# Fifty input projections as twenty-five seven-product units, and a bitwise search for the top 256 on ScalarE

## The chip, the core and the metric

One NeuronCore of a Trainium2 chip runs one program. TensorE (PE) multiplies, with its weight loads (PEld) shown apart; VectorE (DVE), ScalarE (ACT) and GpSimd (POOL) do the rest; SyncE (SP) issues nearly all DMAs. The program holds one list of instructions for each engine; an instruction may name counters of other engines, or of its own, that have to be reached before it starts. The metric is device time in microseconds for one execution, lower is better, taken as the median of several runs.

## The reference, cut to what matters

```python
D_MODEL, SEQ, DEC_BATCH, TOP_K_MAX, Q_BLOCK = 1024, 1024, 8, 256, 128    # T = 8 + 1024 token columns in the kernel
def trunk_layer(x, conv_prev, attend, mem_k, mem_v, lw):
    h = rms_norm(x, g_mix)
    z = jnp.einsum('btd,de->bte', h, w_in)
    (c_in, c_b, c_c, q, k, v, iq, ik, iw, gate_a, gate_b) = jnp.split(z, splits, axis=-1)
    conv_out, conv_state = short_conv(c_c * c_in, conv_prev, conv_w)          # 3 taps
    out_a = jnp.einsum('btc,cd->btd', c_b * conv_out, w_conv_out)
    attn = attend(q, k, v, iq, ik, iw)
    out_b = jnp.einsum('bte,ed->btd', attn, w_attn_out)
    x = x + jnp.einsum('btd,de->bte', sigmoid(gate_a) * out_a + sigmoid(gate_b) * out_b, w_o)
    x = x + memory_attend(rms_norm(x, g_mem), mem_k, mem_v, w_mq, w_mo)
    h = rms_norm(x, g_ffn)
    f = jax.nn.silu(h @ w_gate) * (h @ w_up)
    return x + f @ w_down
def indexer_topk(iq, iw, ik, q_pos, top_k):
    score = einsum('bths,bth->bts', relu(einsum('bthd,bsd->bths', iq, ik)), iw) * IDX_SCALE
    _, idx = lax.top_k(where(causal, score, NEG_INF), top_k)   # attention then sees these 256 keys alone
```

Widths of z in columns: c_in, c_b, c_c, q, gate_a and gate_b 1024 each, k and v 256 each, iq 256, ik 64, iw 4. Everything is float32 to the outside.

## The kernel before

Every float32 operand is held as a high and a low part ("split": ACT copies the high part, POOL or DVE subtracts it to get the low part), and a product is three matmuls: high by high, high by low, low by high. Activations stand transposed, 128 features on the partitions by T = 1032 tokens. SBUF is 48 slots of 1040 floats (`Slots`), handed out in the order in which they came free.

The stages run one after the other on PE: memory keys and values; the index keys and queries ik and iq; nine tiles of v; the index scores of the query blocks 7 to 2 against up to 1024 keys; the input projections; attention; the output and memory-attention products; the feed-forward.

`dense(8, h)` makes one 128-row output of a projection: 8 blocks by 3 products by 3 chunks of 344 columns, 72 matmuls. The input projections are 50 such calls (c_in, c_c and c_b 8 times each, then gate_a, gate_b, k, q), with w_conv_out between them as 32 calls of `dense(2)` that add into eight accumulators (L791). PSUM banks 0 to 5 serve two calls in turn. The results leave PSUM on ACT or DVE after each call; k and q are split and stay in SBUF. After each call `bg.pump(budget)` writes a piece of a background generator into the queues, so many microseconds' worth by costs noted in the generator.

The background work here is `topk()` (L747): for two query blocks at a time 32 rounds of MAX8 (L752) and MATCH_REPLACE8 (L755) on DVE, then a mask. After it comes `sample_index()`, small work for the eight decode tokens. Four index-score pieces of attention (`pre_score`) are hooked into the last q calls.

The feed-forward already uses another form. `unit()` (L1622) makes two 128-row outputs for all 1032 tokens with seven quarter-size products instead of eight (Strassen's scheme in Winograd's form): each product is 4 blocks by 3 matmul kinds by 2 chunks of 258 columns, so a unit is 168 matmuls of 258 columns. It needs sums of quarters of the weights (`UnitWeights.sums`, L226 to L229 on DVE), their splits (`high` L236 on ACT, `low` L244 on DVE) and sums of the activations, made once by `x_sums` and `x_last` (L1586 to L1620). After each of its products 1 to 7 something is taken out of PSUM or prepared for the next unit:

```python
if j == 0:   ACT.copy(c2(half(p1, 0)), psum(0))                 # and split W, Y; load the next unit
elif j == 2: V.tensor_tensor(c2(half(ca, 1)), psum(1), ...)     # bank pair is written again by product 5 (j = 4)
elif j == 3: ACT.copy(...) or V.tensor_tensor(...)              # then UW.sums(u + 1)
elif j == 4: two V.tensor_tensor                                # then UW.high(u + 1, "U")
```

Of the kernel before, what the change touches and what calls it, by code (L numbers as in the profile page):

```python
# [8 lines left out]
F32 = mybir.dt.float32  # L9
# [14 lines left out]
NSLOT = 48  # L24
# [22 lines left out]
def weight_plan():  # L47
# [149 lines left out]
class UnitWeights:  # L197


    def __init__(self, nc, slots, ws):  # L200
        self.nc, self.slots, self.ws = nc, slots, ws
        self.n = ws.shape[0]
# [36 lines left out]
    def low(self, u, x):  # L239
        if u >= self.n:  # L240
            return
        w = 512 if x == "Y" else 1024
        raw, (h,), l = self.raw[u].pop(x), self.hl[u, x], self.slots.get(F32R)
        self.nc.vector.tensor_tensor(l[0][:, :w], raw[0][:, :w], h[0].bitcast(F32)[:, :w], op=ALU.subtract)  # L244
        self.slots.put(raw)
        self.hl[u, x] = h, l

    def operand(self, u, x, q):
        k, i = W_SIDE[x]
        c = 512 * i + 128 * q  # L250
        return [t[0][:, c:c + 128] for t in self.hl[u, k]]
# [64 lines left out]
def build(tc, A):  # L316
# [17 lines left out]
    W = Weights(nc, S, A["ws"])  # L334
    bg = Background()
# [83 lines left out]
    m8 = const.tile([128, 2, 8], F32, name="m8")  # L419
# [77 lines left out]
    def split_ps(ps, between=None):  # L497
# [5 lines left out]
        return h, l  # L503

# [88 lines left out]
    for half in range(2):  # L593
        for kp in range(4):
# [3 lines left out]
            for p in range(3):  # L598
                for kk in range(2):
# [1419 lines left out]
```

## Time and profile before

| | us |
|---|---|
| median of 3 runs (2142.87 to 2146.04) | 2145.67 |
| the profiled execution's own time | 2149.56 |
| its span, first to last instruction | 2147.8 |
| PE busy in the span | 2099.0 |
| DVE, ACT, POOL busy | 1281.1, 621.8, 605.5 |

A dense call is 72 matmuls of 344 columns, a unit 168 of 258 columns. Each view lists instructions under the line of kernel.py that made them; helper lines (L470 for `dense`, L1643 for `unit`) stand for many stages, so stages are told apart by time: v tiles 108 to 134 us, scores 134 to 159, input projections 159 to 790, feed-forward units 1470 to 1881.

### The profile page before, as it was taken

The page shows a single profiled execution, that of the slowest core. Times are in us where ns is not written, and L with a number is a line of the kernel's source. Part 1 is how long each engine was busy: PE and PEld are TensorE (multiplying, and loading weights), DVE is VectorE, ACT ScalarE, POOL GpSimd, SP SyncE. Part 2 cuts the span into 40 slices and gives each one's busy share as a digit, 9 for nine tenths or more (in the row PEclk, how much of TensorE's full clock was granted, in tenths as well). Part 3 has the DMA queues.
Part 4 walks back from the last instruction along what each step waited for, and adds up shares of the span by engine and source line. Part 5 has one row for each costly group of instructions (what it writes and reads, how often), then busy time and mean ns, then how long its engine had stood idle before and what let it go on. Part 6 is the DMA issues. An engine that isn't in the chain of part 4 may idle for free. (4 is left out here: it accounts for less than half of the span.)

```text
span 2147.8 us, 33510 instructions
## 1 busy us (share of the span) xinstructions
PE 2099.0 (98%) x13943; PEld 2037.3 (95%) x13943; DVE 1281.1 (60%) x2155; ACT 621.8 (29%) x933; POOL 605.5 (28%) x393
## 2 busy tenths in 40 slices
PE   8889999999999999999999999999999999999998
PEld 7789999999999998789999988999999999999997
DVE  7658688899975024783223688547777776731114
ACT  5431311211111123673113234244222222232203
POOL 3533222412121223333325353240000000184414
PEclk9999999999999999999999999999999999999999
DMA  7211111111223303006325225321122122262102
GB/s 291 99 50 50 40 50 43 47 50 38 92 78 110 109 7 92 1 1 217 109 89 205 101 89 183 116 88 60 60 99 80 60 99 79 87 240 98 70 1 80
DMA packets 69211, 190.98 MB, mean 89 GB/s; under 512 B 8506, under 2 KB 23170, under 8 KB 69058
## 3 DMA queue, kind: packets, MB, share of 16 engines
q1 hardware_dynamic: 68514, 188.30, 25.2%
q8 instruction: 109, 1.79, 0.4%
q10 hardware_dynamic: 544, 0.53, 0.1%
q14 instruction: 44, 0.36, 0.0%
HBM read 153.54 MB, written 35.26 MB: 88 GB/s over the span
## 5 line engine op out<-in xcount | busy, mean ns | idle before, releaser
L470 PE MATMUL PS<-t,t 128*128 128x344 f32 x8280 | 1314.6, 320 | 3.1 <-DVE t L731 1.3
L470 PEld LDWEIGHTS PS<-t,t 128*128 128x128 f32 x8280 | 1307.2, 188 | 7.2 <-issue 2.1
L169 POOL TENSOR_TENSOR t<-t,t 128x1024 fp32r<-128x1024 f32 x126 | 311.9, 2480 | 486.4 <-ACT t L167 374.9
L1643 PE MATMUL PS<-t,t 128*128 128x258 f32 x3360 | 407.4, 284 | 3.2 <-DVE t L1738 3.2
L1643 PEld LDWEIGHTS PS<-t,t 128*128 128x128 f32 x3360 | 407.2, 191 | 3.4 <-DVE t L1738 3.4
L1573 POOL TENSOR_TENSOR t<-t,t 128x1032 fp32r<-128x1032 f32 x22 | 53.1, 2425 | 425.7 <-ACT t L1572 409.4
L167 ACT ACTIVATE t<-t 128x1024 fp32r<-128x1024 f32 x134 | 139.7, 1050 | 96.0 <-PE PS L470 73.6
L755 DVE MATCH_REPLACE8 t<-m,t 128x1024 f32<-128x1024 f32 (+2 forms) x192 | 166.5, 871 | 0.0
L752 DVE MAX8 m<-t 128x8 f32<-128x1024 f32 (+2 forms) x192 | 162.2, 876 | 0.0
L1822 DVE TENSOR_TENSOR t<-PS,t 128x1032 f32<-128x1032 f32 x32 | 39.5, 1233 | 163.2 <-PE PS L470 163.2
L492 POOL TENSOR_TENSOR t<-t,t 128x1032 fp32r<-128x1032 f32 (+1 forms) x30 | 72.7, 2427 | 186.7 <-ACT t L489 171.3
L1695 DVE TENSOR_TENSOR t<-t,t 128x1032 f32<-128x1032 f32 (+1 forms) x84 | 96.9, 1164 | 2.8 <-ACT t L1724 2.3
L489 ACT ACTIVATE t<-t 128x1032 fp32r<-128x1032 f32 (+2 forms) x32 | 34.0, 1067 | 213.6 <-DVE t L823 82.7
L236 ACT ACTIVATE t<-t 128x1024 fp32r<-128x1024 f32 x80 | 72.0, 948 | 60.2 <-DVE t L226 59.1
L1235 DVE TENSOR_TENSOR t<-PS,t 128x1032 f32<-128x1032 f32 x32 | 39.4, 1232 | 79.1 <-PE PS L470 79.1
L244 DVE TENSOR_TENSOR t<-t,t 128x1024 fp32r<-128x1024 f32 x80 | 85.2, 1086 | 0.0
L1307 DVE CUSTOM_DVE_ANT_0 junk<-t,t 128x256 f32<-128x256 f32 x128 | 75.8, 592 | 9.9 <-ACT t L1349 5.2
L972 POOL TENSOR_SCALAR t<-t,ast 128x128 f32<-128x128 f32 (+7 forms) x64 | 47.8, 747 | 110.3 <-DVE ast L971 81.6
L502 DVE TENSOR_TENSOR t<-PS,t 128x1032 fp32r<-128x1032 f32 x11 | 13.6, 1233 | 98.5 <-ACT t L499 88.6
L991 DVE TENSOR_TENSOR t<-PS,t 128x512 fp32r<-128x512 f32 x72 | 49.6, 688 | 35.5 <-ACT t L987 34.8
L949 PE MATMUL PS<-t,t 128*128 128x512 f32 (+3 forms) x288 | 67.3, 359 | 0.2 <-DVE ast L971 0.2
L999 PE MATMUL PS<-t,t 128*128 128x512 f32 x216 | 64.4, 406 | 0.6 <-DVE t L991 0.4
(255 smaller groups left out, 1808.2 us busy)
## 6 DMA issues: line engine op xcount, KB each, us to landing
t<-in_ws_dram SPq DMA_DIRECT2D x134, 512.0 KB, 4.3
t<-in_wu_dram SPq DMA_DIRECT2D x20, 512.0 KB
t<-in_wu_dram SPq DMA_DIRECT2D x40, 256.0 KB, 3.6
fd<-t SPq DMA_DIRECT2D x18, 516.0 KB, 3.0
t<-fd SPq DMA_DIRECT2D x18, 516.0 KB, 10.4
t<-in_xT_dram SPq DMA_DIRECT2D x16, 516.0 KB, 5.5
t<-in_cmk_dram SPq DMA_DIRECT2D x16, 512.0 KB, 5.7
t<-in_cmv_dram SPq DMA_DIRECT2D x16, 512.0 KB, 5.5
```

The source lines that it names most:

```text
L167: nc.scalar.activation(h[0][:, :1024], raw[0][:, :1024], AF.Copy)
L169: eng.tensor_tensor(l[0][:, :1024], raw[0][:, :1024], h[0].bitcast(F32)[:, :1024], op=ALU.subtract)
L236: self.nc.scalar.activation(h[0][:, :w], self.raw[u][x][0][:, :w], AF.Copy)
L244: self.nc.vector.tensor_tensor(l[0][:, :w], raw[0][:, :w], h[0].bitcast(F32)[:, :w], op=ALU.subtract)
L470: PE.matmul(PS[:, b + c, :CH], w, x[0][:, c * CH:(c + 1) * CH], start=(k == 0 and p == 0), stop=(k == n - 1 and p == 2))
L492: (lo or G).tensor_tensor(l[0][:, :width], src[0][:, :width], hf, op=ALU.subtract)
L752: V.max(m8[:, z, :], sc[i])
L755: V.match_replace(sc[i], m8[:, z, :], sc[i], SENT)
L949: PE.matmul(PS[:, b + c // 512, :w], u[0][:, cs], y[0][:, NS + c:NS + c + w], start=pp == 0, stop=pp == 2)
L1307: V.tensor_tensor_reduce(out=junk, in0=s[0][:, 256 * x:256 * x + 256], in1=rows, scale=1.0, scalar=0.0, op0=ALU.mult, op1=ALU.add, accum_o ...
L1643: PE.matmul(PS[:, banks[z] + c, :HC], a, b[:, HC * c:HC * c + HC], start=j < 3 and q == 0 and p == 0 or j == 5 and q == 0 and p == 0, stop ...
L1695: eng.tensor_tensor(o, o, i, op=ALU.mult)
```

## The change

The fifty dense calls become 25 units. The units run right behind the scores, in the order k, q, gate_a, gate_b, and then four times c_in, c_c, c_b. The activation sums are made earlier for that: `x_sums` for blocks 0 and 1 behind ik, 2 to 5 behind the two iq calls, 6 and 7 behind the first v tile; the first unit's weights are prepared behind the third v tile and the ninth. k, q, both gates after the sigmoid and six of the eight convolution results go to DRAM and come back when needed. w_conv_out is one stage of eight `dense(8)` calls at the end, with the `pre_score` hooks, the loads and the splits of q and k between them. A Y weight quarter keeps both parts in one slot; there are 49 slots.

`topk()` no longer removes maxima. It builds the 256th largest score bit by bit, for six blocks together: per bit it counts the scores below a candidate, five blocks on ACT (Sign with an accumulated sum, written to PSUM banks 6 and 7) and the 384-wide one on DVE, then four small DVE instructions choose the next candidate. After 32 bits a few passes per block on DVE make the mask, with ties resolved by a running count. It is written into the queues by `bg.pump(2.6)` after each of a unit's products.

```diff
-NSLOT = 48
+NSLOT = 49
+MIX_UNITS = 25
     for o in range(8):
-        full("w_in", OFF["ga"], o)
...
+        full("w_conv_out", 0, o)
@@ unit_plan
+    add("w_in", OFF["k"])
+    for part in ("q", "ga", "gb"):
+        for p in range(4):
+            add("w_in", OFF[part] + 256 * p)
+    for p in range(4):
+        for part in ("c_in", "c_c", "c_b"):
+            add("w_in", OFF[part] + 256 * p)
@@ unit(), moved up and given a tick
             for f in side.get(j, ()):
                 f()
             flush()
+            if tick:
+                bg.pump(tick)
@@ behind ik, iq and in the v tiles
+    x_sums(h, GMIX, 0, xs[0], xs[1])
...
+        x_sums(h, GMIX, jt + 1, xs[2 * jt + 2], xs[2 * jt + 3])
...
+        if t == 1:
+            x_sums(h, GMIX, 3, xs[6], xs[7])
+        if t == 3:
+            UW.sums(0)
+            UW.high(0, "U")
+            UW.low(0, "U")
...
+    x_last(h)
+    UW.high(0, "V")
+    UW.low(0, "V")
+    UW.high(0, "W")
@@ topk
-            for r in range(32):
-                for z, i in enumerate((ia, ib)):
-                    V.max(m8[:, z, :], sc[i])
...
-                    V.match_replace(sc[i], m8[:, z, :], sc[i], SENT)
+        for bit in range(31, -1, -1):
+            for n, i in enumerate(TKB):
+                wd = 128 * (i + 1)
+                v = tval[:, n:n + 1]
+                if n < ON_ACT:
+                    ACT.activation(wide[:, :wd], sc[i], AF.Sign, bias=candf[:, n:n + 1], scale=-1.0,
+                                   accum_out=v)
+                else:
+                    V.tensor_scalar(bias2[:, :wd], sc[i], candf[:, n:n + 1], None, op0=ALU.is_lt, op1=ALU.add, accum_out=v)
+                yield (wd + 200) / 1100.0
+            V.tensor_tensor(rej, tval, tlim, op=ALU.is_gt)
+            V.copy_predicated(last_no, rej, cand)
+            V.tensor_scalar(flips, rej, -1.0 if bit == 31 else float(1 << bit), None, op0=ALU.mult)
+            if bit:
+                V.scalar_tensor_tensor(cand, flips, 1 << (bit - 1), cand, op0=ALU.bitwise_xor, op1=ALU.bitwise_xor)
...
+            yield 0.4
+        for n, i in enumerate(TKB):
+            V.tensor_scalar(wide[:, :wd], sc[i], candf[:, n:n + 1], None,
+                            op0=ALU.is_gt, op1=ALU.add, accum_out=tval[:, n:n + 1])
...
+        for n, i in enumerate(TKB):
+            V.tensor_scalar(low, sc[i], t, None, op0=ALU.is_lt, op1=ALU.add, accum_out=tval[:, n:n + 1])
+            V.tensor_scalar(eq, sc[i], t, None, op0=ALU.is_equal)
+            V.tensor_tensor_scan(run, eq, eq, 0.0, op0=ALU.add, op1=ALU.max)
+            V.scalar_tensor_tensor(eq, run, need, eq, op0=ALU.is_gt, op1=ALU.mult)
+            V.tensor_tensor(low, low, eq, op=ALU.add)
+            V.tensor_scalar(low, low, NEG, None, op0=ALU.mult)
@@ the projections
-    for j in range(8):
-        ps = dense(8, h, 8.0)
...
-            conv_out(j // 2 - 1, cvs)
...
+    TICK = 2.6
+    for g, t in enumerate(unit({}, tick=TICK)):
...
+        store(A["o_kT"][g], act(t), t)
+    for m in range(4):
+        for hd, t in enumerate(unit({}, tick=TICK), 2 * m):
...
+            store(qd[hd], act(t), t)
+    for dst in (sad, sbd):
+        for m in range(4):
+            for o, t in enumerate(unit({}, tick=TICK), 2 * m):
+                ACT.activation(act(t), act(t), AF.Sigmoid)
+                store(dst[o], act(t), t)
...
+    for m in range(4):
+        if m == 1:
+            bg.add(sample_index())
+        ia, ib = unit(tail, tick=TICK)
+        ua, ub = unit({}, c11=[ia], tick=TICK)
...
+        ca, cb = unit(join({0: [first], 1: [second]}, last), c11=ya, tick=TICK if m < 3 else 0.0)
...
+    for o in range(8):
...
+        ps = dense(8, cvl, 0.0, hooks)
```

What the scheduler made of it, at three places. First ACT, early in the projections. Before, t is any slot and the rows are the evictions (L798), weight splits (L167), the convolution's first tap (L814) and a split of its result (L489):

```order
L798 ACTIVATE t_1466<-PS 128x1032 [waits DVE_49,PE_49,Activation_49]
L167 ACTIVATE t_1470<-t_792 128x1024 [waits DMAHW6_49,Pool_49]
L809 COPY co<-t_1552 128x2 [waits DVE_49]
L814 ACTIVATE t_1559<-t_1552,cw 128x1024 [waits DVE_49,Pool_49]
L167 ACTIVATE t_1568<-t_883 128x1024 [waits DMAHW0_49,Activation_49]
L489 ACTIVATE t_1650<-t_1559 128x1032 [waits DVE_49,Activation_49]
```

And now, with L603 and L608 the two PSUM copies of a unit, L229 a weight quarter's split and L943 the Sign counts of one bit (widths 1024 to 512), the start of the unit for the first two q heads:

```order
L603 COPY t_1720<-PS 128x516 [waits PE_49]
L229 ACTIVATE t_1750<-t_1607 128x512
L943 ACTIVATE PS,tval<-t_1404,cand 128x512 [waits Activation_49]
L943 ACTIVATE PS,tval<-t_1284,cand 128x1024 [waits DVE_49,Activation_49]
L943 ACTIVATE PS,tval<-t_1311,cand 128x896 [waits Activation_49]
L943 ACTIVATE PS,tval<-t_1342,cand 128x768 [waits Activation_49]
L943 ACTIVATE PS,tval<-t_1373,cand 128x640 [waits Activation_49]
L943 ACTIVATE PS,tval<-t_1404,cand 128x512 [waits Activation_49]
L943 ACTIVATE PS,tval<-t_1284,cand 128x1024 [waits DVE_49,Activation_49]
L608 COPY t_1721<-PS 128x516 [waits PE_49]
```

Each Sign names ACT's own counter, and that of 1024 columns DVE's as well; two ticks of the pump hold exactly one bit, so a unit of seven products holds 3.5 bits between its copies and splits.

Second DVE, from the second iq call to the v tiles. Before, iwc (L680) is the first thing taken out of each v tile's bank:

```order
L663 TENSOR_TENSOR t_961<-PS,t_961 64x1032 [waits DVE_49,Activation_49]
L663 TENSOR_TENSOR t_964<-PS,t_964 64x1032 [waits Activation_49]
L666 COPY iqs<-PS 64x8 x2
L680 TENSOR_SCALAR iwc<-PS 128x4 [waits PE_49] x2
L680 TENSOR_SCALAR iwc<-PS 128x4 [waits PE_49,Activation_49] x7
```

Now, where L539 to L542, L551 and L552 are `x_sums` and L848 is iwc:

```order
L826 COPY iqs<-PS 64x8 x2
L539 TENSOR_TENSOR t_988<-t_105 128x516 [waits Activation_49]
L540 TENSOR_TENSOR t_989<-t_109,t_105 128x516 [waits DMAHW7_49,Activation_49,Pool_49]
L541 TENSOR_TENSOR t_988<-t_109,t_988 128x516 [waits DVE_49]
L542 TENSOR_TENSOR t_989<-t_988,t_109 128x516 [waits DVE_49]
L551 TENSOR_TENSOR t_997<-t_988,t_996 128x1032 [waits Activation_49]
L552 TENSOR_TENSOR t_995<-t_989,t_994 128x516 [waits DMAHW5_49,Activation_49]
L848 TENSOR_SCALAR iwc<-PS 128x4 [waits PE_49]
L539 TENSOR_TENSOR t_1038<-t_113 128x516 [waits Activation_49]
```

Six instructions with two waits for ACT stand ahead of the first v tile's eviction, and the fourth `x_sums` follows at once, ahead of the second tile's.

Third DVE again, where the last bit is known. Before, one round of two blocks, with the eviction of the next PSUM result (L804) behind the MAX8 instructions:

```order
L752 MAX m_157<-t_1208 128x8 [waits DVE_49]
L752 MAX m_157<-t_1235 128x8 [waits DVE_49]
L755 MATCH_REPLACE t_1208<-m_157,t_1208 128x1024 [waits DVE_49]
L755 MATCH_REPLACE t_1235<-m_157,t_1235 128x896 [waits DVE_49]
L752 MAX m_157<-t_1208 128x8 [waits DVE_49]
L752 MAX m_157<-t_1235 128x8 [waits DVE_49]
L804 TENSOR_TENSOR t_1552<-PS,t_1466 128x1032 [waits DMAHW1_49,PE_49,Activation_49]
```

Now the mask of the 1024-wide block (L975 to L986) between the weight sums (L219 to L222) and two evictions (L612, L613) of the unit for the first two gate_b outputs:

```order
L975 TENSOR_SCALAR t_3772,tval<-t_1284,cand 128x1024 [waits DMAHW6_49,DVE_49]
L219 TENSOR_TENSOR t_3699<-t_3698 128x512 [waits DMAHW0_49]
L220 TENSOR_TENSOR t_3700<-t_3699 128x512 [waits DMAHW1_49,DVE_49]
L221 TENSOR_TENSOR t_3698<-t_3699,t_3698 128x512
L222 TENSOR_TENSOR t_3799<-t_3700 128x512 [waits DMAHW7_49,DMAHW2_49,DVE_49]
L979 TENSOR_SCALAR t_3804<-t_1284,cand 128x1024
L980 SCALAR_TENSOR_TENSOR PS<-t_3804 128x1024 [waits DVE_49]
L982 SCALAR_TENSOR_TENSOR need<-tval,PS 128x1 [waits DVE_49]
L983 SCALAR_TENSOR_TENSOR t_3804<-PS,need,t_3804 128x1024 [waits DVE_49]
L612 TENSOR_TENSOR t_3666<-PS,t_3664 128x516 [waits PE_49]
L613 TENSOR_TENSOR t_3666<-PS,t_3666 128x516 [waits DVE_49]
```

The masks of all six blocks stand within ten products of two units, between their evictions and splits.

## Rows read from the trace of the kernel before

**Rows 1.** The page, busy time by engine: us (share) xinstructions.

```profile
PE 2099.0 (98%) x13943; PEld 2037.3 (95%) x13943; DVE 1281.1 (60%) x2155; ACT 621.8 (29%) x933; POOL 605.5 (28%) x393
```

**Rows 2.** Windows of 50 us: length, busy us (instructions) by engine, granted clock, DMA, GB/s.

```profile
100.00:150.00 50.00, 47.31 (x329) 44.75 (x328) 19.78 (x26) 16.52 (x24) 13.71 (x8) 0.98 0.10 32
...
550.00:600.00 50.00, 50.00 (x319) 50.00 (x318) 45.97 (x95) 7.91 (x8) 10.00 (x4) 1.00 0.25 89
...
1550.00:1600.00 50.00, 50.00 (x418) 50.00 (x417) 38.61 (x48) 13.73 (x16) 0.00 (x0) 1.00 0.20 68
```

**Rows 3.** ACT in time: start, duration us; evictions of gate_a and gate_b calls.

```profile
544.14 1.04 ACT L833 ACTIVATE t<-PS 128x1032 f32<-128x1032 f32 x1 [28.82 <-PE PS L470]
...
623.64 1.03 ACT L902 ACTIVATE t<-PS 128x1032 f32<-128x1032 f32 x1 [9.38 <-PE PS L470]
```

**Rows 4.** ACT in time, one feed-forward unit from its first copy to the next unit's.

```profile
1560.67 0.59 ACT L1647 COPY t<-PS 128x516 f32<-128x516 f32 x1 [6.91 <-PE PS L1643]
1561.15 0.64 ACT L236 ACTIVATE t<-t 128x512 fp32r<-128x512 f32 x1
...
1569.81 2.95 ACT L236 ACTIVATE t<-t 128x1024 fp32r<-128x1024 f32 x3
1580.87 0.59 ACT L1647 COPY t<-PS 128x516 f32<-128x516 f32 x1 [8.11 <-PE PS L1643]
```

**Rows 5.** Groups by line: ACT with an accumulated sum, busy us, mean ns, idle before.

```profile
L965 ACT ACTIVATE t<-t,ast 128x1024 f32<-128x1024 f32 x8 | 9.2, 1148 | 5.2 <-DVE ast L959 5.2
...
L965 ACT ACTIVATE t<-t,ast 128x512 f32<-128x512 f32 x8 | 5.9, 733 | 0.0
```

**Rows 6.** ACT in time: such an instruction, its accumulator read, and the next.

```profile
916.35 0.62 ACT L965 ACTIVATE t<-t,ast 128x384 f32<-128x384 f32 x1
916.87 0.19 ACT L965 ACTIVATION_READ_ACCUMULATOR t<-t,ast 128x1 f32 x1
916.96 0.76 ACT L1013 CAST t<-PS 128x128 fp32r<-128x128 f32 x4
```

**Rows 7.** All engines in time: a small DVE instruction and the ACT one that needs it.

```profile
782.69 0.15 DVE L959 TENSOR_SCALAR ast<-ast 128x1 f32<-128x1 f32 x1
782.88 1.15 ACT L965 ACTIVATE t<-t,ast 128x1024 f32<-128x1024 f32 x1 [3.93 <-DVE ast L959]
```

**Rows 8.** DVE in time, in a unit: two weight sums, and two low parts of 1024.

```profile
1567.05 0.68 DVE L226 TENSOR_TENSOR t<-t 128x512 f32<-128x512 f32 x1
1567.77 0.69 DVE L227 TENSOR_TENSOR t<-t 128x512 f32<-128x512 f32 x1
...
1578.60 2.35 DVE L244 TENSOR_TENSOR t<-t,t 128x1024 fp32r<-128x1024 f32 x2
```

**Rows 9.** All engines in time, around the first v tile.

```profile
108.31 26.37 PE L678 MATMUL PS<-t,t 128*128 128x260 f32 x216
...
113.19 0.35 DVE L666 COPY iqs<-PS 64x8 f32<-64x8 f32 x2
113.58 0.16 DVE L680 TENSOR_SCALAR iwc<-PS 128x4 f32<-128x4 f32 x1
```

**Rows 10.** Groups by line: the feed-forward's activation sums on ACT and DVE.

```profile
L1589 ACT ACTIVATE t<-t,gains 128x1032 f32<-128x1032 f32 x8 | 8.8, 1142 | 0.0
...
L1601 ACT ACTIVATE t<-t 128x1032 fp32r<-128x1032 f32 x4 | 4.3, 1068 | 7.8 <-DVE t L1593 7.8
...
L1592 DVE TENSOR_TENSOR t<-t,t 128x516 f32<-128x516 f32 x4 | 2.7, 685 | 0.0
```

**Rows 11.** DVE in time: a mask to bf16, and two three-operand passes of 1032.

```profile
681.08 0.40 DVE L768 TENSOR_SCALAR t<-t 128x512 bf16<-128x512 f32 x1
...
73.82 2.48 DVE L494 SCALAR_TENSOR_TENSOR t<-t,gains,t 128x1032 fp32r<-128x1032 f32 x2
```

**Rows 12.** Windows of 4 us around an idle stretch of PE, columns as in rows 2.

```profile
1472.00:1476.00 4.00, 1.66 (x14) 1.45 (x13) 3.50 (x6) 3.30 (x6) 0.00 (x0) 1.00 0.30 95
1476.00:1480.00 4.00, 3.16 (x14) 3.17 (x15) 4.00 (x6) 1.38 (x3) 0.00 (x0) 0.50 0.64 199
```

More of the change, by code (lines that the diff above doesn't have):

```diff
@@ L503, in split_ps, with load, half, c2 @@
         return h, l
+    def load(src, width=T):
+        s = S.get()
+        nc.sync.dma_start(s[0][:, :width], src)
+        return s
+    UW = UnitWeights(nc, S, A["wu"])
+    def half(s, i):
+        return s[0][:, HT * i:HT * i + HT]
+    def c2(ap):
+        return ap.rearrange("p (c n) -> p c n", n=HC)
+    def split_to(hl, raw, lo, a=0, b=T):
+        h, l = hl
+        ACT.activation(h[0][:, a:b], raw[0][:, a:b], AF.Copy)
+        lo.tensor_tensor(l[0][:, a:b], raw[0][:, a:b], h[0].bitcast(F32)[:, a:b], op=ALU.subtract)
@@ new lines, in x_last, with free_x @@
+    def x_last(hl):
+        for p, e in enumerate(t3):
+            h, l = hl[2 * p]
+            ACT.activation(half(h, 1), half(e, 0), AF.Copy)
+            V.tensor_tensor(half(l, 1), half(e, 0), half(h, 1).bitcast(F32), op=ALU.subtract)
+            S.put(e)
+        t3.clear()
+    def free_x(k):
+        for hl in xslots[k]:
+            put_pairs([hl])
+        xslots[k].clear()
+        for x in {"a": ("B11", "T3"), "b": ("B21", "B22"), "d": ("T1", "T2"), "e": ("T4",)}[k]:
+            X[x] = []
@@ L505, in build, with act, mul, split_slot @@
+    def act(t):
+        return t[0][:, :T]
+    def mul(o, i):
+        V.tensor_tensor(o, o, i, op=ALU.mult)
+    def split_slot(raw, lo):
+        hl = new_pair()
+        split_to(hl, raw, lo)
+        S.put(raw)
+        return hl
+    def join(*ds):
+        out = {}
+        for d in ds:
+            for j, fs in d.items():
+                out.setdefault(j, []).extend(fs)
+        return out
     mh, ml = [S.get(F32R), S.get(F32R)], [S.get(F32R), S.get(F32R)]
@@ L591, in xsplit @@
         h.append(split_sb(xs[k], scale=gain(GMIX, k)))
-    for half in range(2):
+    for hv in range(2):
         for kp in range(4):
@@ L636, in build @@
         xsplit(k)
-    for x in xs:
-        S.put(x)
     S.put(xR)
@@ L826, in build @@
-    store(A["o_conv"], co)
-    ma = dram.tile([8, 128, T], F32, name="ma")
-    sbd = dram.tile([8, 128, T], F32, name="sbd")
-    for o in range(8):
-        ps = dense(8, h, 8.0)
-        t = S.get()
-        ACT.activation(full(t), ps, AF.Sigmoid)
-        if o == 0:
-            conv_out(3, cvs)
-        V.tensor_tensor(full(acc[o]), full(acc[o]), full(t), op=ALU.mult)
-        S.put(t)
-        store(ma[o], acc[o][0][:, :T], acc[o])
+    TKB = (7, 6, 5, 4, 3, 2)
+    ON_ACT = 5
+    cand = const.tile([128, 6], I32, name="cand")
@@ L895, in sample_index @@
         yield 0.4
-    for o in range(8):
-        if o == 1:
-            bg.gens.insert(0, sample_index())
-        ps = dense(8, h, 9.0)
-        t = S.get()
-        ACT.activation(full(t), ps, AF.Sigmoid)
-        store(sbd[o], t[0][:, :T], t)
-    kr = []
-    for g in range(2):
-        ps = dense(8, h, 8.0)
-        t = S.get()
-        ACT.activation(full(t), ps, AF.Copy)
-        kr.append(split_ps(ps))
-        G.tensor_copy(ks_new[:, g, :], t[0][:, 0:NS])
-        store(A["o_kT"][g], t[0][:, :T], t)
+    cst = const.tile([128, 2, NS], F32, name="cst")
@@ L914, in build @@
+    finish()
+    split_cv((4, 5, 6, 7))
+    store(A["o_conv"], co)
+    kr = []
     SCQ = 128 ** -0.5
```

554 lines of the change are left out of this document (295 added, 259 removed).

## Prediction, as written before the change was run

> **What bounds the kernel now.** I read the busy line first: PE is busy for 98% of the span [rows 1]. The windows then say where other engines matter. In the projections (550 to 600 us) PE is busy all 50 us at clock 1.00, DVE 45.97 and ACT 7.91; in the feed-forward units (1550 to 1600) PE again all 50, DVE 38.6, ACT 13.7 [rows 2]. So PE sets the time in both places, DVE has little room in the projections, ACT nearly all of its time. The costs of a call and of a unit come from ACT's list in time: eight evictions from 544.14 to 623.64 enclose seven dense calls, 79.50/7 = 11.357 us each [rows 3]; from the first copy of one unit to that of the next 1580.87 - 1560.67 = 20.20 us, 2.886 per product [rows 4].
>
> The profiled execution took 2149.56 us, 3.9 more than the median of 2145.67. I sum differences on the profiled one and subtract 3.9.
>
> **The gain.** 25 units replace 50 calls: 25 x (2 x 11.357 - 20.20) = **-62.9**. This rests on rows of the same kernel at full clock [rows 3, 4]. w_conv_out keeps its 576 matmuls, sample_index its work on PE: 0. The POOL and ACT splits that go were hidden (ACT 7.9, POOL 10.0 of 50 us [rows 2]): 0, and nothing to win.
>
> **The v tiles.** 216 matmuls in 26.37 us are nine tiles of 2.93, so tiles three and four began at 114.2 and 117.1; DVE finished the iqs copies at 113.5 and then had nothing but 0.16 us instructions [rows 9]. Tiles use two banks in turn, so tile three waits for the eviction of tile one. Now an `x_sums` stands on DVE ahead of that eviction, and another ahead of tile two's. One is a chain between two engines: ACT 2 x 1.142; DVE four half sums at 0.685 [rows 10], each waiting for the last by 0.04 [rows 8]; ACT 1.07 [rows 10]; DVE 1.24 [rows 11] and 0.69; three handovers of 0.04 [rows 7]. That is 2.28 + 2.86 + 1.07 + 1.93 + 0.12 = 8.3 us. Two end at 113.5 + 16.6 = 130.1, tile four starts at 130.3 instead of 117.1: **+13**. Low end: if ACT has done its two multiplications of each before DVE comes to them, 2 x 6.0, so 125.7, +8. [...]
>
> **x_last and the first unit's V and W.** Ahead of the first score evictions now stand ACT 4 x 0.59 + 2 x 0.98 = 4.3 and DVE 4 x 0.69 + 1.2 = 4.0 [rows 4, 8]. DVE and ACT were busy 19.8 and 16.5 us of the 50 around it [rows 2], so some of it may be caught up: bounds 0 and 4.3. I take **+4**, since PE wants the score banks back at once.
>
> **Sign counts.** Two ticks of 2.6 write one bit, two products are 5.77 us of PE, so 32 bits span 64 products = 64 x 2.886 = 184.7 us of PE, 9.14 units. ACT's cost of one bit: the nearest rows are activations with an accumulated sum, 1.148 for 1024 columns and 0.733 for 512 [rows 5]; the next one starts about when the duration ends, 0.61 for 384 columns [rows 6]. Five evenly spaced widths: 5 x (1.148 + 0.733)/2 = 4.70. Then ACT waits for the next candidate: 0.09 until the accumulator read ends [rows 6], 0.04 to DVE, four small instructions at 0.15 [rows 7] with 0.04 between [rows 8], 0.04 back: 0.89. Together 5.59 a bit, 178.9 for 32. ACT's own work in 9.14 units is 9.14 x (2 x 0.59 + 0.64 + 2.95) = 43.6 [rows 4] and eight sigmoids at 1.07 are 8.6 [rows 10]. Sum 231.1 against PE's 184.7: 46.4 too much. ACT may end two products late before PE needs its copy, 5.8 off: **+41**.
>
> Bounds. Each Sign also waits for the one before it. An ACT instruction that doesn't wait starts 0.10 before the accumulator read's end [rows 6], on DVE one that waits for its own engine starts 0.04 after it [rows 8]: 4 x 0.14 = 0.56 a bit more, 64 in all with no lateness allowed. No row shows ACT doing so and none shows a Sign into PSUM, so I take neither this nor a discount. Low: a Sign as cheap as a weight split, (0.983 + 0.64)/2 x 5 = 4.06 [rows 4], and the unit's own copies filling the gap of 0.89: 129.9 + 52.2 = 182.1, below 184.7, so 0. No gain below that: PE is full already.
>
> [...]
>
> **The masks.** From the end of the last bit the rows stand within about 9.5 products, 27.4 us of PE. Seven passes over 4224 elements: three with an accumulated sum, a scan or three operands at 2.48/2 = 1.24 per 1032 [rows 11], 5.1 each; four plain ones at 0.40 per 512 [rows 11], 3.3 each; 2 for small instructions: 30.4. DVE's own work in a unit is four sums at 0.69, lows 3.5 and 0.7 [rows 8], five evictions at 0.69: about 10.5, so 14.3 in 9.5 products. 44.7 - 27.4 = 17.3 too much, less one product of lateness that the banks allow, 2.9: **+14**. Low: two products of lateness and the counting passes as plain ones, +6. High: no lateness, two of the plain passes as dear as the others because they write or read PSUM, about +25.
>
> **The convolution units.** In every third unit from the 13th on, DVE's list after the first product is: a low part 1.2; `first`, 0.69 + five small ones 0.9 + a wait for ACT's tap 0.3 + two passes 2.48 [rows 11]; Y's low 0.7; `second`, the same with a full-width product, 5.05. That is 11.3, then the third product's eviction, 0.69. PE writes that bank again 3 x 2.886 = 8.66 after the first product's end. 11.3 + 0.69 - 8.66 = 3.3 late, four times: **+13**. Low 0 (if work before the third product's end is caught early), high 17 with ACT's 1.07 tap fully in the open.
>
> **Costed at nothing.** The DRAM round trips of q, k, gates and convolution results: DMA is busy 0.25 of the projections [rows 2] and each store or load has many units' time; SP's queue holds stores ahead of the next unit's weight loads, but these are written a unit ahead. Without that cover, a late weight quarter stops PE at a unit's start. The q and k splits behind 11.36 us calls with ACT idle.
>
> **Sum.** -62.9 + 13 + 4 + 41 + 14 + 13 = +22; 2149.6 + 22 - 3.9 = **2168 us**.
>
> **Rivals.** *ScalarE keeps pace.* The bits decide: ACT's term is 0 if a bit costs at most (184.7 + 5.8 - 52.2)/32 = 4.32 us. For it speaks that a plain split is 0.98 and that unit copies may stand in the gap; against, that the row with an accumulated sum is 1.148 and that the chain through DVE cannot begin before the last Sign. The others stay: -62.9 + 13 + 4 + 14 + 13 = -19, **2127**, faster.
> *Cheap Signs, exposed chain.* 4.06 + 0.89 = 4.95 a bit: 158.4 + 52.2 - 190.5 = +20, sum +1, **2147**, no change that can be told: about 0.2%, 4.3 us, is what a measurement of this kernel can tell.
> *ACT waits for DVE, and DVE for PE.* The four small instructions stand on DVE behind an eviction that waits for a product's end; while ACT owes PE a copy or a split, PE's product is late too, and each bit loses a third of a product, 0.96, on top: 32 x 0.96 = +31, **2199**. For it: both lists are fixed. Against: an eviction needed in the middle of a bit is usually over before its chain.
> That the change doesn't do what it says could only be units dearer than 20.20 here; the same 168 matmuls of 258 columns speak against it.
>
> **How the numbers follow.** Forecast (slower, 2152 to 2190) 0.50; ScalarE keeps pace 0.24; cheap Signs 0.14; chained waits 0.12. Faster by over 0.2%: 0.23 of the second, 0.06 of the third, 0.02 of the first, 0.31. Within 0.2%: 0.06 + 0.02, 0.08. Slower: the rest, 0.61. The range leaves out the tails where all small terms lie at their low end beside cheap Signs (below 2114) or all at their high end (above 2200): 2114 to 2200.
>
> **What would show it.** Right: between about 180 and 420 us ACT busy near 100%, first copies of successive units 25 to 27 us apart, PE waiting for ACT's weight highs or copies; after the bits 20.2 us apart; PE idle behind the first v tiles, on DVE; DVE full at the masks. Wrong: 20.2 us spacing during the bits with ACT at 80 to 90%, then 2127 or below; Sign rows of 1024 columns at 0.9 or less; v tiles without a gap. A PE that waits on DMA at unit starts, or runs at clock 0.50 within the units, would be a loss that I have not priced.

## The result and the profile after

The changed kernel takes 2231.09 us (median of 4 runs, 2228.52 to 2234.78) against 2144.35 us for the kernel before, measured beside it: a ratio of 1.0406, 95% interval 1.0388 to 1.0424. It is slower by about 87 us. The forecast had the sign but 2168 us, and its range ended at 2200.

First the page's line of busy time and four windows, with the columns of [rows 1] and [rows 2].

```profile
PE 2084.4 (93%) x14543; PEld 2007.8 (90%) x14543; DVE 1265.4 (57%) x2186; ACT 839.4 (38%) x1347; POOL 463.2 (21%) x333
...
100.00:150.00 50.00, 42.24 (x291) 40.94 (x289) 25.96 (x44) 21.85 (x31) 0.00 (x0) 0.90 0.13 42
200.00:250.00 50.00, 43.38 (x341) 42.53 (x340) 28.02 (x74) 43.98 (x84) 0.00 (x0) 0.97 0.26 85
...
550.00:600.00 50.00, 37.44 (x270) 33.59 (x269) 28.13 (x45) 8.96 (x13) 0.63 (x4) 0.85 0.22 70
...
585.00:609.00 24.00, 9.54 (x29) 2.53 (x27) 1.31 (x6) 0.00 (x0) 0.00 (x0) 0.57 0.18 63
```

PE was full in the projections before. Now it lacks 6.6 us of 50 from 200 on, where ACT (43.98) is the busiest engine, and 12.6 of 50 from 550 on, where none is full. From 585 to 609 hardly anything computes: that is a wait for transfers (the sample scores below), and the prediction had no term for it.

The unit spacings show where it went. These are ACT's first copies of the first, the tenth, the twelfth, and the 16th to 18th unit (start, duration, in time):

```profile
183.29 0.59 ACT L603 COPY t<-PS 128x516 f32<-128x516 f32 x1 [1.95 <-DVE t L242]
...
416.97 0.57 ACT L603 COPY t<-PS 128x516 f32<-128x516 f32 x1
...
477.47 0.59 ACT L603 COPY t<-PS 128x516 f32<-128x516 f32 x1
...
558.42 0.59 ACT L603 COPY t<-PS 128x516 f32<-128x516 f32 x1 [7.14 <-PE PS L599]
583.26 0.59 ACT L603 COPY t<-PS 128x516 f32<-128x516 f32 x1 [9.21 <-PE PS L599]
630.82 0.59 ACT L603 COPY t<-PS 128x516 f32<-128x516 f32 x1 [9.62 <-PE PS L599]
```

Four units from 477.47 to 558.42 are 20.2 us each, as in [rows 4]: the gain is there. Nine units with bits take 233.7 us instead of 181.8, two with masks 60.5 instead of 40.4, one with a convolution 24.84, and one 47.56. Laid out by stage, each against the same stage before or against 20.2 us a unit. The last column is the part in which PE doesn't stand still but takes longer for the same matmuls (its busy time in the stage, less what these matmuls take before, in a unit of 20.2 or, for w_conv_out, in the run e9 below):

| stage | predicted | measured | of it slower matmuls |
|---|---|---|---|
| projections as units | -62.9 | -62.9 (units 20.2 where nothing is added) | |
| ahead of the v tiles | 0 | +1.4 | 0.3 |
| v tiles | +13 | +10.6 | 3.4 |
| scores | +4 | +7.6 | 4.0 |
| first unit's first product | 0 | +1.8 | 1.8 |
| bits | +41 | +51.9 | 20.0 |
| masks | +14 | +20.1 | 1.4 |
| convolution units | +13 | +18.6 | 7.0 |
| sample scores (47.56 - 20.2 - 4.4 that before paid too) | 0 | +23.0 | 7.1 |
| w_conv_out | 0 | +7.3 | 2.3 |
| sum | +22 | +79.4 | 47.3 |

The slower matmuls go with the clock: the granted clock averages 0.79 in the scores (0.93 before), 0.60 in the first product, 0.96 in the bits and 1.00 in the four plain units. The spans differ by 81.5, so about 2 us are without a row. From the first matmul of attention on, the two traces keep their distance (80.8 us there, 81.5 at the end).

### The profile page after: what moved, and what is told of

Read it like the earlier page. It is cut to its first block, busy times and chain, and to the rows that moved or that the text cites. A ratio compares the mean times of both kernels' runs of the same rounds, so it can differ in the third digit from the quotient of the medians.

```text
span 2229.3 us, 35300 instructions
## 1 busy us (share of the span) xinstructions
PE 2084.4 (93%) x14543; PEld 2007.8 (90%) x14543; DVE 1265.4 (57%) x2186; ACT 839.4 (38%) x1347; POOL 463.2 (21%) x333
## 5 line engine op out<-in xcount | busy, mean ns | idle before, releaser
L599 PE MATMUL PS<-t,t 128*128 128x258 f32 x7560 | 945.9, 288 | 70.0 <-DVE t L605 24.9
L599 PEld LDWEIGHTS PS<-t,t 128*128 128x128 f32 x7560 | 938.2, 194 | 77.8 <-DVE t L605 26.9
L470 PE MATMUL PS<-t,t 128*128 128x344 f32 x4680 | 748.6, 321 | 7.9 <-POOL t L162 5.5
L162 POOL TENSOR_TENSOR t<-t,t 128x1024 fp32r<-128x1024 f32 x76 | 190.8, 2516 | 260.0 <-ACT t L160 230.8
L229 ACT ACTIVATE t<-t 128x1024 fp32r<-128x1024 f32 (+1 forms) x180 | 163.4, 946 | 127.4 <-DVE t L219 100.0
L242 DVE TENSOR_TENSOR t<-t,t 128x1024 fp32r<-128x1024 f32 (+1 forms) x180 | 192.5, 1084 | 24.2 <-ACT t L229 24.2
L943 ACT ACTIVATE PS<-t,cand 128x1024 f32<-128x1024 f32 (+4 forms) x160 | 144.2, 901 | 26.7 <-DVE cand L952 24.0
L160 ACT ACTIVATE t<-t 128x1024 fp32r<-128x1024 f32 x84 | 87.7, 1051 | 79.7 <-PE PS L470 43.4
L603 ACT COPY t<-PS 128x516 f32<-128x516 f32 x45 | 26.4, 586 | 241.8 <-PE PS L599 231.5
L1587 DVE CUSTOM_DVE_ANT_0 caus<-t,t 128x256 bf16<-128x256 f32 x128 | 77.2, 603 | 10.0 <-ACT t L1629 5.2
L489 ACT ACTIVATE t<-t 128x1032 fp32r<-128x1032 f32 (+2 forms) x24 | 25.5, 1067 | 132.7 <-DVE t L1499 77.0
L520 ACT ACTIVATE t<-t 128x1032 fp32r<-128x1032 f32 x40 | 41.5, 1060 | 85.3 <-PE PS L470 45.0
L608 ACT COPY t<-PS 128x516 f32<-128x516 f32 x27 | 15.7, 582 | 152.2 <-PE PS L599 152.2
```

The lines of the kernel that those rows point to most:

```text
L160: nc.scalar.activation(h[0][:, :1024], raw[0][:, :1024], AF.Copy)
L162: eng.tensor_tensor(l[0][:, :1024], raw[0][:, :1024], h[0].bitcast(F32)[:, :1024], op=ALU.subtract)
L229: self.nc.scalar.activation(h[0][:, :w], self.raw[u][x][0][:, :w], AF.Copy)
L242: self.nc.vector.tensor_tensor(l[0][:, o:o + w], raw[0][:, :w], h[0].bitcast(F32)[:, :w], op=ALU.subtract)
L470: PE.matmul(PS[:, b + c, :CH], w, x[0][:, c * CH:(c + 1) * CH], start=(k == 0 and p == 0), stop=(k == n - 1 and p == 2))
L599: PE.matmul(PS[:, banks[z] + c, :HC], a, b[:, HC * c:HC * c + HC], start=j < 3 and q == 0 and p == 0 or j == 5 and q == 0 and p == 0, stop ...
```

## Experiments

Each starts from the changed kernel, 2231.09 us, unless it says otherwise; times are medians. The kernel before, run beside each of them, gave 2142.85 to 2147.41, so a few us of a difference mean nothing.

### The sample scores

```diff
-        yield 1.0
+        for _ in range(8):
+            yield 2.6
         yield None
```

> The only change: between sample_index's sixteen loads and its first matmul the pump writes eight more products of the units, instead of one. Theory (PE's list puts the sample-score matmuls 2.9 us behind loads that SP needs 19.3 us to issue, so PE stands still): the unit of 47.6 us falls to about 20.5 and the total by 25 to 27 us, to about 2205. Rival (SP itself is late because it also has the units' weight loads, and the unit would wait for its weights anyway): PE then waits on a DMA at the next unit instead, the total falls by less than 10, to 2221 or more.

Measured: 2212.21, 18.9 less. The stretch in the changed kernel (SP issues, PE matmuls):

```profile
586.70 19.33 SPq L1017 DMA_DIRECT2D t<-in_ci_dram  x16
...
590.22 1.03 PE L1026 MATMUL PS<-t,t 64*32 64x257 f32 x2 [4.11 <-DMA t<-in_ci_dram]
...
607.81 1.03 PE L1026 MATMUL PS<-t,t 64*32 64x257 f32 x2 [1.70 <-DMA t<-in_ci_dram]
```

With eight more products between the loads and the matmuls:

```profile
585.11 19.33 SPq L1017 DMA_DIRECT2D t<-in_ci_dram  x16
...
607.62 3.65 PE L1027 MATMUL PS<-t,t 64*32 64x257 f32 x16
```

The sixteen loads take SP the same 19.33 us, but PE comes to them 22.5 us after the first instead of 3.5, and its sixteen matmuls run in 3.65 us in one piece. The kernel before had the same 19.8 us of issues, hidden behind whole dense calls:

```profile
626.16 19.79 SPq L863 DMA_DIRECT2D t<-in_ci_dram  x16
...
L872 PE MATMUL PS<-t,t x16: 377/377/401, 646.2 to 649.5; 64*32 64x257 f32 x16
```

The theory holds, though less than its 25 to 27 came back: the matmuls and sample_index's small instructions on DVE now fall into the next two units, 27.7 and 26.9 us instead of 20.2 and 25.1.

### The bits: spread, unchained, or left out

```diff
-    TICK = 2.6
+    TICK = 1.8
```

> The only change: the pump's budget behind each product is 1.8 instead of 2.6, so a bit of the search is spread over three products (8.7 us of PE) instead of two (5.8). Theory (ACT has too much to do: 6.05 us a bit and 4.8 of its own per unit): per three products 6.05 + 2.05 = 8.1 us of ACT against 8.7 of PE, so units come 20.2 to 21 us apart during the bits, the masks are spread too and lose under 8 instead of 20; about 60 us less, 2170. Rival (each bit costs PE a fixed stall, since the chain through DVE and the copies hold each other up, however far apart the bits are): 32 bits cost the same 52 us over more units, only the masks gain, 2215 to 2225.

Measured: 2183.54, 47.6 less. The window from 200 us on, with the budget of 1.8:

```profile
200.00:250.00 50.00, 50.00 (x418) 50.00 (x417) 32.19 (x79) 45.58 (x86) 0.00 (x0) 1.00 0.38 127
```

PE is full and ACT is busier than in the changed kernel (45.58 against 43.98), as three products leave it 8.66 us for 8.1 of work. The rival, a fixed stall per bit, would have left the 52 us. Not all of the theory's 60 came: the gate units with bits still take 20.9 to 25.4, which their two sigmoids, 2.1 us more on ACT, may explain, and the units with the masks, now the 12th to the 14th, take 24.0, 29.4 and 21.0.

```diff
-                    ACT.activation(wide[:, :wd], sc[i], AF.Sign, ...)
+                    ACT.activation(two[n % 2][:, :wd], sc[i], AF.Sign, ...)   # halves of a bf16 slot
```

> The only change: the Signs write their (unused) result as bf16 to two halves of an SBUF slot in turn instead of f32 to one PSUM region, so a Sign no longer waits for the one before it. Theory (that wait is what made a bit 6.05 us instead of the 5.59 predicted): starts of successive Signs come 0.1 us closer, a bit takes 5.5 to 5.7 us, and 32 bits on an ACT that is the bound give back 10 to 17 us: 2214 to 2221. Rival (SBUF as destination costs more than it saves, or the spacing is set by the accumulator read, not by the wait): spacing within 0.03 us of before, time 2228 to 2236.

Measured: 2221.07, 10.0 less. One bit on ACT in the changed kernel, with nothing else between (start, duration):

```profile
212.18 1.12 ACT L943 ACTIVATE PS<-t,cand 128x1024 f32<-128x1024 f32 x1 [0.77 <-DVE cand L952]
213.23 0.19 ACT L943 ACTIVATION_READ_ACCUMULATOR PS<-t,cand 128x1 f32 x1
213.45 1.01 ACT L943 ACTIVATE PS<-t,cand 128x896 f32<-128x896 f32 x1
...
216.64 0.69 ACT L943 ACTIVATE PS<-t,cand 128x512 f32<-128x512 f32 x1
217.27 0.19 ACT L943 ACTIVATION_READ_ACCUMULATOR PS<-t,cand 128x1 f32 x1
218.23 1.12 ACT L943 ACTIVATE PS<-t,cand 128x1024 f32<-128x1024 f32 x1 [0.77 <-DVE cand L952]
```

And with two destinations:

```profile
210.31 1.15 ACT L944 ACTIVATE t<-t,cand 128x1024 bf16<-128x1024 f32 x1 [0.78 <-DVE cand L953]
211.36 0.19 ACT L944 ACTIVATION_READ_ACCUMULATOR t<-t,cand 128x1 f32 x1
211.46 1.03 ACT L944 ACTIVATE t<-t,cand 128x896 bf16<-128x896 f32 x1
...
215.79 1.15 ACT L944 ACTIVATE t<-t,cand 128x1024 bf16<-128x1024 f32 x1 [0.78 <-DVE cand L953]
```

A Sign that waits for its forerunner starts 0.03 us behind the end of the accumulator read (213.42 to 213.45), one that doesn't 0.09 ahead of it (211.55 to 211.46). A bit goes from 6.05 to 5.48 us. The spacing says the wait and not the read sets it. The total fell at the small end of the theory's 10 to 17. Only 83 of the 160 Signs stand right behind another Sign (46 follow a copy or a split, 31 wait for DVE's candidate), so the wait is worth 83 x 0.13 = 10.6 us and not 32 x 0.57 = 18; the destination changed too, and each Sign got 0.02 us longer.

```diff
-        for bit in range(31, -1, -1):
+        for bit in range(0, -1, -1):
```

> Leaves out 31 of the search's 32 bits, so the counts of one bit and the masks are all that is left of it; everything else stands as in the changed kernel. Theory (the bits cost what the unit spacings say, 51.9 us from the first unit's copy to the tenth's over 20.2 each): the units of the bits fall to 20.2 and the total to about 2231 - 50 = 2181, the masks now lying in the first two units and costing their 20. Rival (part of the spacing is the sigmoids and stores of the gates, or the units themselves are dearer here than 20.2): units without bits stay above 21, total above 2195.

Measured: 2181.44, 49.7 less, against 51.9 read from the spacings. The copies of its second to fourth unit:

```profile
212.62 0.59 ACT L603 COPY t<-PS 128x516 f32<-128x516 f32 x1 [12.29 <-PE PS L599]
248.49 0.59 ACT L603 COPY t<-PS 128x516 f32<-128x516 f32 x1 [11.39 <-PE PS L599]
268.71 0.59 ACT L603 COPY t<-PS 128x516 f32<-128x516 f32 x1 [8.09 <-PE PS L599]
```

The units behind the masks take 20.2 us in the place of the gates too, so neither sigmoids nor stores cost anything by themselves: the bits did, with the sigmoids on top of an ACT already full. In the 233.7 us of the bits in the changed kernel ACT is busy 206.9 and waits 24.0 for the next candidate, and has hardly any other idle time. The masks, now in the first two units, cost 24.

### The v tiles

```diff
-        if t == 1:
-            x_sums(h, GMIX, 3, xs[6], xs[7])
+        next(xsteps, None)      # a quarter of x_sums 2, then of 3, ahead of each tile
```

> The only change: the activation sums of blocks 4 to 7 are written in four steps each, one step ahead of each v tile, instead of as two whole chains ahead of the evictions of tiles one and two. Theory (PE waits for the tiles' two banks because a whole chain stands ahead of an eviction): the nine v tiles take 27 us instead of 37, PE doesn't wait more than 0.5 us among them, and the total falls by 9 to 11: about 2221. Rival (DVE and ACT have too much to do from ik to the scores, so work that is moved shows up as waits of the scores): the scores get later by what the tiles gain, total 2228 to 2234.

Measured: 2219.12, 12.0 less. PE in time, changed kernel and then this one (L846 and L854 are the v tiles, L893 and L903 the scores):

```profile
109.67 5.91 PE L846 MATMUL PS<-t,t 128*128 128x260 f32 x48
120.63 4.77 PE L846 MATMUL PS<-t,t 128*128 128x260 f32 x24 [5.05 <-ACT t L856]
127.57 19.10 PE L846 MATMUL PS<-t,t 128*128 128x260 f32 x144 [2.17 <-ACT t L856]
146.51 2.96 PE L893 MATMUL PS<-t,t 128*128 128x512 f32 x12
```

```profile
109.67 5.91 PE L854 MATMUL PS<-t,t 128*128 128x260 f32 x48
115.96 8.94 PE L854 MATMUL PS<-t,t 128*128 128x260 f32 x72 [0.38 <-ACT t L864]
125.38 11.80 PE L854 MATMUL PS<-t,t 128*128 128x260 f32 x96 [0.48 <-ACT t L864]
137.01 2.96 PE L903 MATMUL PS<-t,t 128*128 128x512 f32 x12
```

The two waits are gone, the tiles take 27.3 us instead of 36.8, and the scores behind them keep their 32 us: the work was not too much, it stood in the wrong place.

### Masks and convolutions

```diff
-                yield (wd + 200) / 960.0      # and the four other costs of the mask passes
+                yield (wd + 200) / 436.4
```

> The only change: the costs that the pump takes for the passes of the masks are 2.2 times as large, so the same passes stand over some 21 products instead of 9.5. Theory (30 us of masks and 14 of its own work stand on DVE in 27 us of PE): the two units of 32.8 and 27.7 us become three or four of 20.5 to 23, and the total falls by 11 to 17: 2214 to 2220. Rival (each long pass ahead of an eviction costs PE its own time, however far apart the passes are): the loss is spread and keeps its sum, total 2227 to 2234.

Measured: 2219.93, 11.2 less. The units of 32.8, 27.7 and 20.2 us become 24.4, 26.8 and 19.2. Some stays, as the passes are dearer than I had them (below).

```diff
-        ca, cb = unit(join({0: [first], 1: [second]}, last), ...)
+        ca, cb = unit(join({0: [first], 4: [second]}, last), ...)
```

> The only change: in every third unit from the 13th the second convolution column (second) is written behind the fifth product instead of the second. Theory (first and second, 9.5 us on DVE, stand ahead of the third product's eviction, which PE needs at 8.7): the four units of 24.8 us become 20.5 to 22.5, total 8 to 16 less, 2215 to 2223. Rival (DVE has 20 us of work in such a unit of 20.2, so what is moved is late at a later product): these units stay above 24, total 2227 to 2234.

Measured: 2232.72, no gain. The four units take 23.9, 23.1, 24.6 and 23.4 instead of 24.8, 25.1, 24.9 and 21.8 (the last to its end). PE's wait in the first of them:

```profile
577.62 6.62 PE L599 MATMUL PS<-t,t 128*128 128x258 f32 x40 [2.52 <-DVE t L242]
```

PE no longer waits for the third product's eviction, but for DVE's low parts of the next unit's weights (L242). My theory fell; the rival is right that DVE has too much in that unit. The little that the first three units gained is no gain of the edit either: they take 23.3, 23.4 and 24.8 with the budget of the masks alone changed (e5); the last section has such a unit in two runs.

```diff
+        # m in (1, 2): {0: [first]} here, and in the unit behind it {1: [second], 4: [finish]}
```

> The only change: for the second and third of the four convolution units, second is written in the following unit (behind its second product) and finish behind that unit's fifth product. Theory (such a unit is late because DVE has 20 us of work in it, and the next one has 9.7 to spare): the units of 25.1 and 24.9 us become 20.2 to 20.5, total 8 to 10 less, 2221 to 2223. Rival (DVE's order ahead of the third product's eviction decides, so first alone still makes it late): they stay above 22, total 2226 or more.

Measured: 2220.47, 10.6 less. The units of 25.1 and 24.9 are 20.3 and 20.2: work has to leave the unit, not move within it.

### w_conv_out

```diff
-    W.sahead = 1
+    W.sahead = 2
```

> The only change: in w_conv_out a weight block is split one call earlier (sahead 2 instead of 1). Theory (PE waits there for POOL's low parts and ACT's high parts, 7 us in the stage, because a block's split is written in the call ahead of it and stands behind other work): no wait for a weight split in the stage, total 5 to 8 less, 2223 to 2226. Rival (what is late is POOL itself, which also has v's and k's splits and the softmax there): the waits move to attention, total 2228 to 2234.

Measured: 2219.78, 11.3 less, more than the 7.3 read from the stage. The three places in the changed kernel where PE's dense calls waited there for a split:

```profile
878.74 3.56 PE L470 MATMUL PS<-t,t 128*128 128x344 f32 x21 [1.40 <-POOL t L162]
...
891.79 1.21 PE L470 MATMUL PS<-t,t 128*128 128x344 f32 x6 [0.68 <-ACT t L160]
895.89 5.02 PE L470 MATMUL PS<-t,t 128*128 128x344 f32 x21 [2.90 <-POOL t L162]
```

With the split a call earlier there is no wait and the stage ends after 97.6 us instead of 104.9: 5.0 of waits, and 2.3 of slower matmuls behind them (the last row has 21 in 5.02 us, the first in 3.56). The rival is out. Of the other 4 us, 3.0 lie in two convolution units that the edit doesn't touch, 23.3 and 23.6 instead of 24.8 and 25.1 (last section); the rest is within what medians here spread.

### Together

> All five changes tried alone, together: budget 1.8 behind a product, Signs into two halves in turn, sample loads six products ahead, activation sums spread over the v tiles, mask passes at 1.5 times their cost, second behind the fifth product. Theory (the losses lie in different places and add up): from 2231 the parts 47, 19, 12, and 5 to 10 each of what is left of the Signs, masks and convolutions come off, 2130 to 2142, so about the kernel before. Rival (the bits now reach into the convolution units, where DVE has no room, and the sums don't add up): 2150 to 2165.

Measured: 2155.45, ratio 1.0053 (1.0036 to 1.0070). The rival's range: the single gains do not add up. The first fourteen units, with bits and masks, take 308.5 us and took 313.1 with the budget of 1.8 alone: the Signs into halves and the spread masks, 10.0 and 11.2 by themselves, add only 4.6 to it, and two units with masks are left at 29.4 and 23.6. The last unit ends on second moved late, with PE waiting 6.17 us.

> As the one with all five together, but the pump's overdraft is carried to the next product and the budget is 2.2 in k, q, c_in and c_c units, 2.0 in gate units, 1.2 in the units with the convolution, so that ACT has 2.9 us or less per product in each; and the low parts of w_conv_out come from DVE instead of POOL. Theory (ACT and DVE set a unit's time only where they have more than 20.2 us to do): no unit above 22 us but the two with the sample scores, w_conv_out's 7 us of waits gone, 2105 to 2125, faster than both kernels. Rival (what remains are stalls of order, not of load, which a finer budget does not touch): the same as with all five, or up to 10 us less.

Measured: 2164.62, which neither theory had. The units end 15 us earlier than with all five, but w_conv_out is worse by more, 129.9 us against 107.4. What its matmuls and weight loads waited for, both counted (us, times):

```profile
  DVE t L162: 41.5, 14
```

PE itself is idle for 20.4 us of the stage. DVE's low parts for a block stand behind the eviction of the call before, and the block's first matmul needs them at once. On POOL that split ran beside the evictions (in the changed kernel for 2.41 us from 876.27, with an eviction of 1.23 at 876.44).

> As the one with budgets by unit (2.2, 2.0, 1.2, overdraft carried), but the low parts of w_conv_out are back on POOL and prepared one call earlier; in two of the four convolution units second stands in the next unit and finish behind it, in the last one second is back behind the second product; and the first unit's V is split in that unit, not ahead of the scores. Theory (DVE's 20 us in a convolution unit, a split that comes in the same call, and work ahead of the scores are what is left): 8 less from the two convolution units, 6 at the last unit's end, 25 to 30 from w_conv_out against the split on DVE, 2 ahead of the scores, 2110 to 2125, faster than both kernels. Rival (the stalls move on to attention, which waits for loads and splits issued in w_conv_out): 2135 or more.

Measured: 2113.94, ratio 0.9842 (0.9818 to 0.9866) against 2147.41 of the kernel before beside it: faster than both. Two windows of it, one with bits and one in the convolutions:

```profile
200.00:250.00 50.00, 50.00 (x418) 50.00 (x417) 32.63 (x79) 43.66 (x85) 0.00 (x0) 1.00 0.35 115
550.00:600.00 50.00, 50.00 (x417) 50.00 (x416) 34.12 (x51) 11.94 (x17) 0.63 (x4) 1.00 0.23 71
```

ACT does as much in the first as in the changed kernel (43.66 and 43.98 us), and PE stands still for none of it. The page's line of busy time:

```profile
PE 2043.9 (97%) x14543; PEld 1975.6 (94%) x14543; DVE 1268.9 (60%) x2186; ACT 828.4 (39%) x1347; POOL 464.8 (22%) x333
```

The 14543 matmuls are those of the changed kernel, which had PE busy 2084.4 us with them: with most of the waits gone, PE also needs 40.5 us less for the same work. The idea of the change carried a gain all along, 33 of the 63 us here; its order did not.

## Why the prediction was wrong

**Right:** the gain (units of 20.2 us); that ScalarE becomes the bound in the bits (e2, e7) and that this, the v tiles, the masks and the convolutions eat the gain; the sign. *ScalarE keeps pace* and *cheap Signs* are out: the units were 24.6 to 28 us apart. So are the chained waits: ACT waited for DVE's candidate 31 times and 24.0 us in all, 0.77 each, as in the bit shown above, with no third of a product on top.

**The step that failed most** is the sentence "w_conv_out keeps its 576 matmuls, sample_index its work on PE: 0". The work is the same, the cover is not. The pump used to be called once in 11.36 us and is now called once in 2.886, so the one `yield None` between loads and matmuls, which ends what the pump writes at a time, is worth a quarter of what it was; SP's 19.3 us of issues were bare. 23 us (15.8 with PE idle, 7.1 in slower matmuls), of which e1 took 18.9 off. The same sentence hides the 7.3 us of w_conv_out, where a block is now split in the call ahead of its use, beside the splits of v and the pieces of pre_score (e9). A PE that waits on a DMA was named as a loss not priced; the place to price it was the distance of each load from its use.

**The clock behind the waits** is the other term at nothing. The rows had it, with 0.50 in [rows 12], and the prediction named a clock of 0.50 within the units as a loss not priced. It came: of the 144 us that the change loses, its gain of 62.9 aside, 47 are slower matmuls (last column of the table). The 20 in the bits are covered, as ACT sets the pace there; the 27 in the other stages stand in their sums.

**Bits, 41 for 52.** I left out the wait of a Sign for the one before it because no row of ACT showed it; with it the prediction named 64 in all, but carried that into neither the sum nor the range. It was there: 6.05 us for a bit with nothing between, against 5.59 computed without it and 6.15 with it, and e3 took off 0.57. Over all 32 bits it is 10.6 us, and 41 and 10.6 make the 51.9. The chain through DVE was as summed: 0.90 from the end of the last Sign (217.33) to the next candidate's first (218.23), against 0.89.

**Masks, 14 for 20.** Of the seven passes four and not three are of the dear kind (two counts, the scan, the three-operand pass), and the scan was counted at 1.24 us per 1032 columns:

```profile
427.70 1.28 DVE L975 TENSOR_SCALAR_CACHE_REDUCE t<-t,cand 128x1024 bf16<-128x1024 f32 x1
...
431.44 0.75 DVE L979 TENSOR_SCALAR t<-t,cand 128x1024 bf16<-128x1024 f32 x1
432.22 2.30 DVE L980 TENSOR_TENSOR_SCAN PS<-t 128x1024 f32<-128x1024 bf16 x1
...
434.74 1.28 DVE L983 SCALAR_TENSOR_TENSOR t<-PS,need,t 128x1024 bf16<-128x1024 f32 x1
```

A scan takes 2.30 us, nearly twice what I took: 9.8 for the six blocks instead of 5.1. All passes together took DVE 38.8 us instead of 30.4; with that the prediction's sum gives 22.8. The high end of 25 held it. For its plain passes that touch PSUM the kernel before has a row, 1.28 us for 1024 columns from PSUM to SBUF (L731, f32) against 0.68 from SBUF to SBUF (L768, to bf16); what of that is the place and what the type was not shown. No plain pass of the masks touches PSUM in the changed kernel, and its counts took 1.28 into PSUM (L961, f32) as into SBUF (L975, bf16).

**Convolutions, 13 for 18.6.** The rows were as listed: the third product's eviction starts at 569.13, 10.7 us after the unit's first DVE product at 558.43. PE waited there for 2.82 us, and for 3.0, 2.9 and 2.9 in the other three, against the 3.3 of the sum, so the wait was priced rightly. What the step missed are the 7.0 us of slower matmuls behind these waits. It also looked at one eviction alone: e6 showed that with this one free, another wait for DVE takes its place.

**v tiles, 13 for 10.6, and scores, 4 for 7.6**, have the right cause; the sizes are in part luck. The tiles' two waits are 7.2 us, well under 13, and slower matmuls bring them near it. In the scores PE waits 3.6 us more than before, within the bound of 4.3, and 4.0 of slower matmuls carry them over it.

**The range** missed by 31 us because all its ends belonged to terms that I had listed. For the v tiles no run shows a high end above the 13 of the sum; they took 10.6, of which 3.4 in slower matmuls. With 13 there and every other term at its highest, the 64 for the bits included, the sum is 2206. Terms at nothing had no upper end, and sample scores and w_conv_out alone were 30 us.

## What to carry to other kernels

When a call that drives background work becomes shorter, every distance that is counted in calls shrinks with it: look through each generator for loads and splits that lie one step ahead of their use. Before pricing an engine's work, ask how much of it fits under the engine that bounds the kernel in the same stretch; here the counts cost 52 us in nine units, and in the last kernel the first twelve units together took 8 us more than 20.2 each. A step "at nothing" deserves an upper end of its own, and each wait of PE a price for the matmuls behind it, here 27 us of slower matmuls in the stages other than the bits.

## What was not expected of the hardware

A Sign of 1024 columns took 1.12 us into PSUM (f32, the changed kernel) and 1.15 into SBUF (bf16, e3), one of 896 columns 1.01 and 1.03. The two also differ in type, so no run here shows the destination alone.

Two DVE passes of 1024 columns took 2.61 us in a convolution of the changed kernel:

```profile
566.61 2.61 DVE L1085 SCALAR_TENSOR_TENSOR t<-t,cw,t 128x1024 f32<-128x1024 f32 x2 [0.55 <-ACT t L1080]
```

and 4.61 at the end of the last unit in the run of all five changes together, where POOL ran a split beside them:

```profile
715.93 4.61 DVE L1098 SCALAR_TENSOR_TENSOR t<-t,cw,t 128x1024 f32<-128x1024 f32 x2 [0.60 <-ACT t L1093]
...
716.93 2.53 POOL L162 TENSOR_TENSOR t<-t,t 128x1024 fp32r<-128x1024 f32 x1 [2.15 <-ACT t L160]
```

In the changed kernel POOL ran nothing beside the two passes. Whether its split made the difference was not shown: no run here took it apart.

While PE waited for the sample loads, from 585 to 609 us, its granted clock averaged 0.57 (the window above), and the sample matmuls took 601 to 632 ns against 377 in the kernel before:

```profile
L1026 PE MATMUL PS<-t,t x16: 601/618/632, 590.2 to 608.2; 64*32 64x257 f32 x16
```

So this wait of PE was paid twice, the second time in the matmuls behind it. Not every wait was: this is the first convolution unit in the changed kernel and then in e9, whose edit lies elsewhere (columns as in [rows 2]):

```profile
567.00:571.00 4.00, 1.18 (x10) 1.13 (x10) 3.96 (x5) 0.00 (x0) 0.00 (x0) 1.00 0.00 0
571.00:575.00 4.00, 4.00 (x23) 4.00 (x23) 2.62 (x6) 2.95 (x3) 0.00 (x0) 0.57 0.00 0
```

```profile
567.00:571.00 4.00, 1.18 (x10) 0.98 (x9) 3.96 (x5) 0.00 (x0) 0.00 (x0) 1.00 0.00 0
571.00:575.00 4.00, 4.00 (x36) 4.00 (x35) 3.48 (x6) 2.96 (x3) 0.00 (x0) 1.00 0.00 0
```

PE waited as long in both, ten matmuls in 4 us. Over the next 4 us the granted clock averaged 0.57 in the one, with 23 matmuls, and 1.00 in the other, with 36; the unit took 24.84 us and 23.31. Why they differ is not shown here.
